# First expert weight blocks in half-block buffers, and another order of the last pieces and the second norm

## The chip, the core and the metric

One program on one core of a Trainium2 chip. The metric is the device time of one execution in microseconds (us). The engines are PE (TensorE, with PEld its weight loads), DVE (VectorE), ACT (ScalarE), POOL (GpSimd) and SP (SyncE, which here only issues transfers).

## What is computed

One layer of a hybrid encoder on 512 tokens of width 1024, in float32: three token mixers (chunk-band attention, gated delta rule, causal pooling), gated, merged and projected; a residual sum and a layer norm; then a mixture of experts, a residual sum and a second layer norm. The change touches only the second half:

```python
x = layer_norm(DN_ALPHA * x + mix, ln1_g[i], ln1_b[i])
ffn = hierarchical_moe(x, ...)      # top group of 4, then top 2 of its 8 experts, per token
x = layer_norm(DN_ALPHA * x + ffn, ln2_g[i], ln2_b[i])

def expert_block(args):             # 32 experts; w1, w3: 1024x512, w2: 512x1024
    xb, e = args
    hdn = jax.nn.silu(xb @ w1[e]) * (xb @ w3[e])
    return hdn @ w2[e]

def layer_norm(x, g, b):
    mu = jnp.mean(xf, axis=-1, keepdims=True)
    var = jnp.mean(jnp.square(xf - mu), axis=-1, keepdims=True)
    return ((xf - mu) * lax.rsqrt(var + LN_EPS) * g + b)
```

## The kernel before

**The expert stage.** All 32 experts are computed, each for up to 64 tokens that chose it. They are taken in 16 pairs; the two experts of a pair stand in the two 64-column halves of the PE array. The tokens of four experts are gathered by matmuls with one-hot matrices (`gather`, group "g" in the profile). Per pair there are three products: with w1 and with w3 (`first_product`, 8 chunks of the contraction by 2 experts, output `as`), silu and multiplication (`gated`), four transposes of the result (`turned_slots`, output `g`), and with w2 (`product`, output `pj`). Each float32 matmul of these stands in the trace as two, so one first product is 32 rows and one second product 32 rows of 512 columns or 64 of 256. The loop over the pairs runs w1 of pair `pr`, then w2 of pair `pr - 1`, then w3 of pair `pr`.

**The weights.** One expert matrix is a block of 2 MB; there are 96 blocks, and a pair uses two blocks per product. They pass through eight slots of one block each, in one fixed arena of on-chip memory. Every buffer in the program is a name for a range of that arena (`reg(offset, size)`), and two names may overlap. `seq` holds the order of use: blocks 0 and 1 are w1 of pair 0, 2 and 3 its w3, 4 and 5 w1 of pair 1, 6 and 7 w2 of pair 0, 8 and 9 w3 of pair 1, and so on. `load_expert` issues blocks 0 to 5 as one transfer each, blocks 7 and 8 in quarters, `load_quarter` block 6 in quarters; these go out while the mixers still run. From block 9 on `load_parts` issues half a block (1 MB, line 1098) or a whole one (2 MB, line 1094) into whatever `done_with` has declared free. In pairs 0 to 2 a slot's first half is declared free in the middle of a product, after chunk 4 of 8, or for w2 after the second of four 256-column pieces (`PIECES`).

**What sets the order.** From `held(True)` on, PE, ACT and DVE each run strictly in the order in which the program text issues; SP issues its transfers in one queue in the order of issue, each after its own waits. Waits come from overlaps: a read of a buffer waits for earlier writes to any buffer that overlaps it.

**The end.** Pairs 13 to 15 are not written out, but combined on chip: `product` leaves a high part (ACT) and a low part (DVE, `m_512r` or `m_1024r`), `combine` multiplies both with a token matrix and adds the result to the residual `yacc`, for four token tiles. For pair 15 that addition also gives the row sum of each 256-column piece, and a pass with Square gives its sum of squares: on ACT, and for the last piece of tiles 2 and 3 on DVE. `gained(k)` multiplies piece `k` by the norm's gain in place. `second_scale(t)` makes mean and 1/deviation of one tile (nine small instructions on three engines), `second_norm(t)` applies them and stores the rows.

```python
def block(i):                        # before: blocks 0 to 5
    return lambda c: reg(slot(i), 8, 512)[:, c]
```

Of the kernel before, what the change touches and what calls it, by code (L numbers as in the profile page):

```python
# [14 lines left out]
AF = mybir.ActivationFunctionType  # L15
OP = mybir.AluOpType
# [145 lines left out]
def body(tc, T):  # L162
# [24 lines left out]
    pool, sp = nc.gpsimd, nc.sync  # L187
# [9 lines left out]
    def reg(off, *dims, r=False):  # L197

        n = math.prod(dims)
        key = (off, n, r)  # L200
        if key not in placed:
            name = "m%d_%d%s" % (off, n, "r" if r else "")
            placed[key] = nc.alloc_sbuf_tensor_at(name, [128, n], F32R if r else F32, offset=base + 4 * off)
        v = placed[key][:, 0:n]
        return shaped(v.bitcast(F32) if r else v, *dims)

    def shaped(v, *dims):
        if len(dims) == 1:
            return v
        names = "abcd"[:len(dims)]  # L210
        kw = {names[i]: dims[i] for i in range(len(dims) - 1)}
        return v.rearrange("p (%s) -> p %s" % (" ".join(names), " ".join(names)), **kw)

    r32 = lambda v: v.bitcast(F32R)

    def pt(tag, bufs, *dims):
        t = ps.tile([128, 512], F32, name=tag, tag=tag, bufs=bufs)
        if not dims:
            return t
        return shaped(t[:, :math.prod(dims)], *dims)  # L220
# [39 lines left out]
    ident = C["ident"]  # L260
# [765 lines left out]
    def slot(i):  # L1026

        return YHL[0] if i == 0 else YO if i == 6 else slots[i - 1 - (i > 6)]

    def quarter(i, k):  # L1030

        return reg(RING[2] + 1024 * k if i == 7 else woh[1][k], 1024)
# [6 lines left out]
    def block(i):  # L1039

        if seq[i][0] == "moe_w2":
            if i == 7:
                return lambda f, cs: shaped(quarter(i, cs.start // 256), 4, 256)[:, f]
            if i > 8:
                return lambda f, cs: w2_columns(shaped(half(i, cs.start // 512), 2, 4, 256), f,
                                                slice(cs.start % 512, cs.start % 512 + cs.stop - cs.start))
            return lambda f, cs: w2_columns(reg(slot(i), 4, 4, 256), f, cs)
        if i == 8:
            return lambda c: quarter(i, c // 2)[:, c % 2 * 512:c % 2 * 512 + 512]
        if i > 8:  # L1050
            return lambda c: shaped(half(i, c // 4), 4, 512)[:, c % 4]
        return lambda c: reg(slot(i), 8, 512)[:, c]

    def blocks(pr):
# [18 lines left out]
    def half(i, h):  # L1073

        p = place_of[i]
        return reg(p[0], 4096)[:, 2048 * h:2048 * h + 2048] if i in whole else reg(p[h], 2048)
# [48 lines left out]
    def load_expert(i=None):  # L1125
        if i is None:
            i = nl_[0]
            nl_[0] += 1
        if i == 8:

            for p in range(4):
                for k in (7, 8):
                    sp.dma_start(quarter(k, p), T[seq[k][0]][seq[k][1]][:, 1024 * p:1024 * p + 1024])
        elif i < 6:
            sp.dma_start(reg(slot(i), 4096), T[seq[i][0]][seq[i][1]])

    def load_quarter(t):

# [392 lines left out]
    def combine(pr, cs, PT_, ws):  # L1531

        n = cs.stop - cs.start
        pcs = [pt(*((("pj", 3), ("ao", 1), ("pj", 3), ("g", 2)) if pr == 13 else
                    (("as", 2), ("ao", 1), ("as", 2), ("g", 2)))[t])[:, :n] for t in range(4)]

        for t in range(4):
            for i, v in enumerate(outs(pr, cs)):
                pe.matmul(pcs[t], r32(PT_[:, t]), r32(v), start=(i == 0), stop=(i == 1))
            ya, pc = yacc[:, t, cs], pcs[t]  # L1540
            if pr < 15:
                dve.tensor_tensor(ya, ya, pc, op=OP.add)
            else:

                k = cs.start // n
                dve.scalar_tensor_tensor(ya, pc, 1.0, ya, op0=OP.mult, op1=OP.add, accum_out=bnp[:, t, k, 1:2])
                if k == 3 and t > 1:
                    d = sil[1][:, (t % 2) * n:(t % 2) * n + n]
                    dve.tensor_scalar(d, ya, -float(n), bnp[:, t, k, 1:2], op0=OP.mult, op1=OP.add)
                    dve.scalar_tensor_tensor(d, d, 1.0, d, op0=OP.mult, op1=OP.mult, accum_out=bnp[:, t, k, 2:3])  # L1550
                else:
                    act.activation(junk[:, :n], ya, AF.Square, scale=-float(n), bias=bnp[:, t, k, 1:2],
                                   accum_out=bnp[:, t, k, 2:3])

    def gained(k, ts=range(4)):

        for t in ts:
            ya = yacc[:, t, PIECES[k]]
            dve.tensor_tensor(ya, ya, late["g2"][:, PIECES[k]], op=OP.mult)
# [14 lines left out]
    bnp = bns.rearrange("p t a b -> p t (a b)")[:, :, 0:3 * len(PIECES)].rearrange("p t (k b) -> p t k b", b=3)  # L1574
    junk = sil[0]

    def second_scale(t):

        ms, rows2 = late["ms"], late["rows"]
        dve.bn_aggr(mv[:, t], bnp[:, t].rearrange("p a b -> p (a b)"))  # L1580
        act.activation(mv[:, t, 1:2], mv[:, t, 1:2], AF.Sqrt, scale=256.0 ** -2, bias=eps[:, 1:2])
        yield
        m, d = mv[:, t, 0:1], mv[:, t, 1:2]
        dve.reciprocal(d, d)
        dve.tensor_scalar(r32(ms[:, t, 0:3:2]), m.to_broadcast([128, 2]), d, None, op0=OP.mult)
        dve.tensor_scalar(ms[:, t, 1:2], m, d, ms[:, t, 0:1], op0=OP.mult, op1=OP.subtract)
        p = pt("g", 2)[0:5, 0:128]
        pe.transpose(p, ms[:, t, 0:5], ident)
        act.activation(r32(rows2[:, t]), p, AF.Copy)
        yield  # L1590

    def second_norm(t):

# [54 lines left out]
    for pr in range(16):  # L1648
# [15 lines left out]
        if 0 < pr < 15:  # L1664
            for cs in PIECES if pr == 1 else halves:
                product(pr - 1, cs, blocks(pr - 1)[4:], *turned_.get(pr - 1, ()))
                if pr < 3 and cs.stop == 512:
                    done_with(pr - 1, "moe_w2", hs=(0,))
            done_with(pr - 1, "moe_w2", hs=(1,) if pr < 3 else (0, 1))
            if pr < 14:  # L1670
                put_rows(pr - 1)
            else:
                for cs in halves:
                    combine(pr - 1, cs, *turned_[pr - 1])
# [46 lines left out]
    dve.memset(late["ms"][:, :, 3:5], 1.0)  # L1721
    last[2]()
    next(rows_)
    combine(14, halves[1], *turned_[14])
    next(rows_)
    last[3]()
    combine(15, PIECES[0], *turned_[15])
    last[4]()
    combine(15, PIECES[1], *turned_[15])
    gained(0)  # L1730
    last[5]()
    combine(15, PIECES[2], *turned_[15])
    gained(1)
    combine(15, PIECES[3], *turned_[15])
    scales = [second_scale(t) for t in range(4)]
    for t in range(6):
        if t < 4:
            next(scales[t])
        if 0 < t < 5:
            next(scales[t - 1])  # L1740
        if t < 4:
            gained(2, (t,))
            gained(3, (t,))
        if t > 1:
            second_norm(t - 2)
    ctx.close()


# [14 lines left out]
```

## Time and profile before

| what | value |
|---|---|
| runs | 1113.26, 1115.53, 1116.07 us; median 1115.53 |
| profiled execution | 1114.25 us, span of the trace 1112.5 us |
| mean granted PE clock | 0.956 of full |
| busy in the span | PE 1010.5 us (91%), DVE 467.2, ACT 310.1, POOL 193.1 |
| HBM read | 254.67 MB |

The page of the profile has busy time by engine, slices of the span, transfer queues, the chain that ended last and groups of instructions. "Idle before, releaser" is the time an engine stood before an instruction and what ended that wait. The granted clock is the share of its full rate that PE was given; 1.0 is 2.4 GHz and 0.5 is 1.2 GHz. The DMA share is the mean busy share of the core's 16 transfer engines. Line 182 (and 180) is a helper through which all PE, DVE and ACT instructions go.

### The profile page before, as it was taken

The page shows a single profiled execution, that of the slowest core. Times are in us where ns is not written, and L with a number is a line of the kernel's source. Part 1 is how long each engine was busy: PE and PEld are TensorE (multiplying, and loading weights), DVE is VectorE, ACT ScalarE, POOL GpSimd, SP SyncE. Part 2 cuts the span into 40 slices and gives each one's busy share as a digit, 9 for nine tenths or more (in the row PEclk, how much of TensorE's full clock was granted, in tenths as well). Part 3 has the DMA queues.
Part 4 walks back from the last instruction along what each step waited for, and adds up shares of the span by engine and source line. Part 5 has one row for each costly group of instructions (what it writes and reads, how often), then busy time and mean ns, then how long its engine had stood idle before and what let it go on. Part 6 is the DMA issues. An engine that isn't in the chain of part 4 may idle for free. (4 is left out here: it accounts for less than half of the span.)

```text
span 1112.5 us, 13291 instructions
## 1 busy us (share of the span) xinstructions
PE 1010.5 (91%) x5174; PEld 647.9 (58%) x5174; DVE 467.2 (42%) x1010; ACT 310.1 (28%) x651; POOL 193.1 (17%) x182
## 2 busy tenths in 40 slices
PE   8989996999999999999976599989899899988893
PEld 5778785977677888887761253525243453523352
DVE  6766993257744524434660111141111152122647
ACT  6883332255743223342240010101010010100023
POOL 1631650132330101331230000000012000001000
PEclk9999998999999999999987899999999899998986
DMA  9422314311114233344663769999999999999952
GB/s 350 141 85 67 114 38 114 108 32 52 39 42 156 107 114 132 152 152 175 265 229 121 295 241 411 425 426 428 428 425 427 428 425 422 426 425 426 417 243 76
DMA packets 44354, 266.40 MB, mean 239 GB/s; under 512 B 15096, under 2 KB 15608, under 8 KB 24448
## 3 DMA queue, kind: packets, MB, share of 16 engines
q1 hardware_dynamic: 39920, 254.53, 57.3%
q0 software_dynamic: 3504, 8.49, 2.0%
q10 hardware_dynamic: 864, 2.49, 0.7%
q8 instruction: 42, 0.69, 0.2%
q14 instruction: 24, 0.20, 0.0%
HBM read 254.67 MB, written 14.09 MB: 242 GB/s over the span
## 5 line engine op out<-in xcount | busy, mean ns | idle before, releaser
L182 PE MATMUL as<-m,m 128*64 128x512 f32 x1024 | 253.7, 627 | 32.3 <-DMA m<-moe_w 31.5
L180 PE MATMUL pj<-m_4096r,m_1024r 128*128 128x512 f32 x800 | 253.1, 396 | 0.0
L182 PEld LDWEIGHTS as<-m,m 128*64 128x64 f32 x1024 | 76.0, 144 | 186.9 <-issue 140.9
L180 PE MATMUL pj<-m_4096r,m_2048r 128*128 128x512 f32 x448 | 170.1, 397 | 9.7 <-ACT m_2048r L180 5.5
L180 PEld LDWEIGHTS pj<-m_4096r,m_1024r 128*128 128x128 f32 x800 | 147.0, 188 | 33.8 <-issue 4.5
L182 PE MATMUL pj<-m,m 128*64 128x512 f32 (+1 forms) x608 | 122.9, 546 | 10.8 <-DMA m<-moe_w 10.8
L180 ACT ACTIVATE m_1024r<-m 128x512 fp32r<-128x512 f32 (+1 forms) x90 | 78.2, 869 | 145.2 <-PE pj L180 120.4
L180 DVE TENSOR_TENSOR m_2048r<-m,m_1024r 128x1024 fp32r<-128x1024 f32 x67 | 76.4, 1141 | 97.7 <-ACT m_1024r L180 97.6
L180 PEld LDWEIGHTS pj<-m_4096r,m_2048r 128*128 128x128 f32 x448 | 85.0, 190 | 29.6 <-ACT m_2048r L180 5.5
L182 PEld LDWEIGHTS pj<-m,m 128*64 128x64 f32 x608 | 48.4, 143 | 80.8 <-issue 68.7
L180 PE MATMUL g<-m,m 128*128 128x128 f32 (+5 forms) x472 | 68.7, 281 | 14.8 <-DMA m<-dx 11.0
L182 DVE COPY m<-pj 128x512 f32<-128x512 f32 (+1 forms) x14 | 9.1, 653 | 172.8 <-PE pj L182 172.8
L1511 POOL DMA_INDIRECT yd<-m,m x13 | 12.6, 968 | 373.2 <-DVE m L182 339.4
L180 PEld LDWEIGHTS g<-m,m 128*128 128x128 f32 (+3 forms) x472 | 58.6, 173 | 27.9 <-issue 16.0
L182 DVE TENSOR_TENSOR m<-m,as 128x512 f32<-128x512 f32 x20 | 13.7, 686 | 139.9 <-PE as L182 139.9
L182 ACT ACTIVATE m<-g 128x512 f32<-128x512 f32 x16 | 9.6, 597 | 176.1 <-PE g L182 176.1
L182 PE MATMUL g<-m_1024r,m_4096r 128*128 128x256 f32 x224 | 55.0, 287 | 0.0
L182 PE MATMUL g<-m_1024r 128*128 128x256 f32 x224 | 54.0, 283 | 0.0
L783 POOL TENSOR_SCALAR m<-m,m 128x128 f32<-128x128 f32 (+3 forms) x32 | 36.6, 1152 | 90.8 <-DVE m L180 84.9
L180 PE MATMUL pj<-m_1024r,m_4096r 128*128 128x512 f32 (+1 forms) x204 | 50.4, 391 | 0.6 <-ACT m_4096r L180 0.6
L182 ACT ACTIVATE m<-g,m 128x256 f32<-128x256 f32 x28 | 15.8, 564 | 116.7 <-PE g L182 116.7
L182 PEld LDWEIGHTS g<-m_1024r,m_4096r 128*128 128x128 f32 x224 | 42.9, 191 | 7.3 <-issue 6.5
(205 smaller groups left out, 1263.8 us busy)
## 6 DMA issues: line engine op xcount, KB each, us to landing
m<-moe_w SPq DMA_DIRECT2D x70, 2048.0 KB, 22.9
m<-moe_w SPq DMA_DIRECT2D x44, 1024.0 KB, 18.3
m<-wm SPq DMA_DIRECT2D x33, 1024.0 KB, 4.9
m<-moe_w SPq DMA_DIRECT2D x16, 512.0 KB, 6.0
yd<-m SPq DMA_DIRECT2D x4, 1024.0 KB, 8.3
m<-wo SPq DMA_DIRECT2D x2, 2048.0 KB, 10.2
m<-yd POOLq DMA_DIRECT2D x8, 512.0 KB, 29.7
m<-xT SPq DMA_DIRECT2D x8, 256.0 KB, 6.2
```

Of the source, the lines that this page charges most:

```text
L180: return f(*args, **kw)
L182: r = f(*args, **kw)
L783: pool.tensor_scalar(s_[:, :n], s_[:, :n], st[:, 1:2], None, op0=OP.mult)
L1511: pool.indirect_dma_start(out=yd, out_offset=bass.IndirectOffsetOnAxis(ap=tabs.bitcast(I32)[:, pr, 0:1], axis=0), in_=ybf[pr], in_offset=N ...
```

## The change

It has five parts. (1) Blocks 1 to 5 are loaded as two transfers of 1 MB into two buffers of half a block, and read through these names. (2) The two w2 blocks of pair 0 are declared free in one go after the last of the four pieces; before, their first halves after the second piece. (3) At the end, the second half of `combine(14)` moves from before the second piece of pair 15 to after the first `gained`; the last piece's product moves behind the third piece's `combine`; `gained(2)` is done for all tiles before the last piece. (4) The squares of the last piece of tiles 2 and 3 move from DVE to ACT. (5) The scales of the second norm are made for all four tiles in one set of instructions.

```diff
@@ block(i)
+        if i:
+            return lambda c: reg(slot(i) + 2048 * (c // 4), 4, 512)[:, c % 4]
         return lambda c: reg(slot(i), 8, 512)[:, c]
@@ load_expert
+        elif i == 0:
+            sp.dma_start(reg(slot(i), 4096), T[seq[i][0]][seq[i][1]])
         elif i < 6:
-            sp.dma_start(reg(slot(i), 4096), T[seq[i][0]][seq[i][1]])
+            for h in range(2):
+                sp.dma_start(reg(slot(i) + 2048 * h, 2048), T[seq[i][0]][seq[i][1]][:, 2048 * h:2048 * h + 2048])
@@ combine, pair 15
-                if k == 3 and t > 1:
-                    d = sil[1][:, (t % 2) * n:(t % 2) * n + n]
-                    dve.tensor_scalar(d, ya, -float(n), bnp[:, t, k, 1:2], op0=OP.mult, op1=OP.add)
-                    dve.scalar_tensor_tensor(d, d, 1.0, d, op0=OP.mult, op1=OP.mult, accum_out=bnp[:, t, k, 2:3])
-                else:
-                    act.activation(junk[:, :n], ya, AF.Square, scale=-float(n), bias=bnp[:, t, k, 1:2],
-                                   accum_out=bnp[:, t, k, 2:3])
+                act.activation(junk[:, :n], ya, AF.Square, scale=-float(n), bias=bnp[:, t, k, 1:2],
+                               accum_out=bnp[:, t, k, 2:3])
@@ second_scale(t) becomes second_scales()
+        for t in range(4):
+            dve.bn_aggr(mv[:, t], bnp[:, t].rearrange("p a b -> p (a b)"))
+        m, d = mv[:, :, 0:1], mv[:, :, 1:2]
+        act.activation(d, d, AF.Sqrt, scale=256.0 ** -2, bias=eps[:, 1:2])
         dve.reciprocal(d, d)
+        dve.tensor_tensor(r32(ms[:, :, 0:3:2]), m.to_broadcast([128, 4, 2]), d.to_broadcast([128, 4, 2]), op=OP.mult)
+        dve.tensor_tensor(ms[:, :, 1:2], m, d, op=OP.mult)
+        dve.tensor_tensor(ms[:, :, 1:2], ms[:, :, 1:2], ms[:, :, 0:1], op=OP.subtract)
+        p = pt("g", 2, 4, 128)
+        for t in range(4):
+            pe.transpose(p[0:5, t], ms[:, t, 0:5], ident)
+        act.activation(r32(rows2), p[0:5], AF.Copy)
@@ loop over pairs
-                if pr < 3 and cs.stop == 512:
+                if pr == 2 and cs.stop == 512:
                     done_with(pr - 1, "moe_w2", hs=(0,))
-            done_with(pr - 1, "moe_w2", hs=(1,) if pr < 3 else (0, 1))
+            done_with(pr - 1, "moe_w2", hs=(1,) if pr == 2 else (0, 1))
@@ the end
     next(rows_)
-    combine(14, halves[1], *turned_[14])
+    last[3]()
     next(rows_)
-    last[3]()
     combine(15, PIECES[0], *turned_[15])
     last[4]()
     combine(15, PIECES[1], *turned_[15])
     gained(0)
-    last[5]()
+    combine(14, halves[1], *turned_[14])
     combine(15, PIECES[2], *turned_[15])
     gained(1)
+    gained(2)
+    last[5]()
     combine(15, PIECES[3], *turned_[15])
-    scales = [second_scale(t) for t in range(4)]
...
+    gained(3)
+    second_scales()
+    for t in range(4):
+        second_norm(t)
```

The first place is PE in the w1 product of pair 0, chunks 3 to 5. A name like `m27648_4096_62` is a buffer at offset 27648 of 4096 elements, number 62; `m14336_4096_109` is block 0, the buffer at 27648 (and 29696) block 1, and `DMAHW6_49` the semaphore of a transfer. Before:

```order
L182 MATMUL as_4355<-m14336_4096_109,m20480_2048_121 64x512 [waits Activation_49]
L182 MATMUL as_4355<-m27648_4096_62,m20480_2048_121 64x512
L182 MATMUL as_4355<-m14336_4096_109,m20480_2048_121 64x512 [waits DVE_49]
L182 MATMUL as_4355<-m27648_4096_62,m20480_2048_121 64x512 [waits DMAHW6_49]
L182 MATMUL as_4355<-m14336_4096_109,m20480_2048_121 64x512 [waits Activation_49]
L182 MATMUL as_4355<-m27648_4096_62,m20480_2048_121 64x512
```

and with the change:

```order
L182 MATMUL as_4360<-m14336_4096_109,m20480_2048_121 64x512 [waits Activation_49]
L182 MATMUL as_4360<-m27648_2048_134,m20480_2048_121 64x512
L182 MATMUL as_4360<-m14336_4096_109,m20480_2048_121 64x512 [waits DVE_49]
L182 MATMUL as_4360<-m29696_2048_3744,m20480_2048_121 64x512 [waits DMAHW2_49]
L182 MATMUL as_4360<-m14336_4096_109,m20480_2048_121 64x512 [waits Activation_49]
L182 MATMUL as_4360<-m29696_2048_3744,m20480_2048_121 64x512
```

At chunk 4 the matmul on block 1 waited on semaphore 6; now it reads a buffer of its own, at 29696, and waits on semaphore 2, that of the transfer that fills it.

To the same place belongs SP's queue at the loads from block 9 on, as it stood before. A transfer waits for the last user of the semaphore that it takes:

```order
L1098 DMA m18432_2048_110<-moe_w3 128x2048 [waits DMAHW4_49]
L1140 DMA m10240_4096_173<-moe_w2 128x1024 [waits DVE_49,DMAHW5_49,PE_49,Pool_49]
L1098 DMA m27648_2048_134<-moe_w3 128x2048 [waits DMAHW6_49,PE_49]
L1098 DMA m48128_2048_314<-moe_w1 128x2048 [waits DMAHW7_49,PE_49]
L1098 DMA m44032_2048_63<-moe_w1 128x2048 [waits DMAHW0_49,PE_49]
L1098 DMA m50176_2048_3243<-moe_w1 128x2048 [waits DMAHW1_49,PE_49]
```

Semaphore 6 belongs to the third row, the second half of block 9, which goes into offset 27648, the first half of block 1's slot. The next rows (semaphores 7, 0, 1) are halves of blocks 10 and 11 into the slots of blocks 2 and 3. With the change the same six rows stand there in the same order.

The second place is SP's queue at the first expert loads. Before:

```order
L278 DMA m48128_2048_314<-wm 128x2048 [waits DMAHW7_49,DVE_49,PE_49]
L278 DMA m44032_2048_63<-wm 128x2048 [waits DMAHW0_49,DMAHW6_49,DVE_49,PE_49]
L1135 DMA m48128_4096_3744<-moe_w3 128x4096 [waits DMAHW4_49,DVE_49,PE_49]
L1135 DMA m27648_4096_62<-moe_w1 128x4096 [waits DMAHW2_49,PE_49,Pool_49]
L1135 DMA m44032_4096_3746<-moe_w3 128x4096 [waits DMAHW3_49,DMAHW6_49,DVE_49,PE_49]
L1135 DMA m35840_4096_3291<-moe_w1 128x4096 [waits DMAHW1_49,DVE_49,PE_49]
```

and with the change:

```order
L278 DMA m48128_2048_314<-wm 128x2048 [waits DMAHW7_49,DVE_49,PE_49]
L1140 DMA m50176_2048_3243<-moe_w3 128x2048 [waits DMAHW6_49,DVE_49,PE_49]
L278 DMA m44032_2048_63<-wm 128x2048 [waits DMAHW0_49,DVE_49,PE_49]
L1140 DMA m48128_2048_314<-moe_w3 128x2048 [waits DMAHW1_49,DMAHW4_49,DVE_49,PE_49]
L1140 DMA m29696_2048_3744<-moe_w1 128x2048 [waits DMAHW2_49,Pool_49]
L1140 DMA m27648_2048_134<-moe_w1 128x2048 [waits PE_49]
L1140 DMA m46080_2048_233<-moe_w3 128x2048 [waits DMAHW3_49,DMAHW5_49,DVE_49,PE_49]
L1140 DMA m44032_2048_63<-moe_w3 128x2048 [waits DMAHW6_49,DMAHW7_49,DVE_49,PE_49]
```

Ten half loads stand in the place of five whole ones, and the second half of block 2 (offset 50176) now stands ahead of the last mixer weights (line 278, offset 44032).

The third place is DVE at the end, from the sum of a piece on. `m_4096_173` is `yacc`; the additions of `as`, `ao`, `as`, `g` over 128x512 are the second half of `combine(14)`, those over 128x256 with a second output a piece of pair 15, and the 128x256 products with `m_1024_4241` (`m_1024_4246`) are `gained`. Before:

```order
L182 TENSOR_TENSOR m_4096_173<-m_4096_173,as 128x512
L182 TENSOR_TENSOR m_4096_173<-m_4096_173,ao 128x512
L182 TENSOR_TENSOR m_4096_173<-m_4096_173,as 128x512
L182 TENSOR_TENSOR m_4096_173<-m_4096_173,g 128x512
L182 SCALAR_TENSOR_TENSOR m_1024r<-m_1024r,m_2048_60,m_1024_4245 5x1024
L182 SCALAR_TENSOR_TENSOR m_1024r<-pj,m_976_61,m_1024r 128x256
L182 SCALAR_TENSOR_TENSOR m_4096_173,m_976_61<-as,m_4096_173 128x256
L182 SCALAR_TENSOR_TENSOR m_4096_173,m_976_61<-ao,m_4096_173 128x256
L182 SCALAR_TENSOR_TENSOR m_4096_173,m_976_61<-as,m_4096_173 128x256
L182 SCALAR_TENSOR_TENSOR m_4096_173,m_976_61<-g,m_4096_173 128x256
L182 SCALAR_TENSOR_TENSOR m_1024r<-pj,m_976_61,m_1024r 128x256
L182 SCALAR_TENSOR_TENSOR m_4096_173,m_976_61<-as,m_4096_173 128x256
```

and with the change:

```order
L182 TENSOR_TENSOR m_4096_173<-m_4096_173,m_1024_4246 128x256 x4
L182 TENSOR_TENSOR m_4096_173<-m_4096_173,as 128x512
L182 TENSOR_TENSOR m_4096_173<-m_4096_173,ao 128x512
L182 TENSOR_TENSOR m_4096_173<-m_4096_173,as 128x512
L182 TENSOR_TENSOR m_4096_173<-m_4096_173,g 128x512
L182 SCALAR_TENSOR_TENSOR m_4096_173,m_976_61<-as,m_4096_173 128x256
L182 SCALAR_TENSOR_TENSOR m_4096_173,m_976_61<-ao,m_4096_173 128x256
L182 SCALAR_TENSOR_TENSOR m_4096_173,m_976_61<-as,m_4096_173 128x256
L182 SCALAR_TENSOR_TENSOR m_4096_173,m_976_61<-g,m_4096_173 128x256
L182 TENSOR_TENSOR m_4096_173<-m_4096_173,m_1024_4246 128x256 x8
L182 SCALAR_TENSOR_TENSOR m_1024r<-pj,m_976_61,m_1024r 128x256
L182 SCALAR_TENSOR_TENSOR m_4096_173,m_976_61<-as,m_4096_173 128x256
```

The four additions of `combine(14)` stood ahead of the low part of the second piece; now they stand between the first `gained` and the third piece, and eight `gained` products stand ahead of the low part of the last piece.

## Rows read from the trace of the kernel before

**Rows 1.** Page, part 2: DMA busy share in 40 slices of 27.8 us.
```profile
DMA  9422314311114233344663769999999999999952
```

**Rows 2.** Two stretches: length, busy us by engine, granted clock, DMA share, GB/s.
```profile
581.90:651.40 69.50, 48.12 (x198) 17.66 (x197) 6.09 (x20) 4.39 (x8) 2.59 (x3) 0.80 0.53 201
651.40:1060.30 408.90, 379.04 (x1890) 167.92 (x1888) 102.00 (x240) 40.46 (x72) 26.75 (x30) 0.97 0.99 418
```

**Rows 3.** Timeline of PE from the first expert product: start, us, work, idle before and releaser.
```profile
581.88 4.50 PE L182 MATMUL as<-m,m 128*64 128x512 f32 x18
...
590.60 9.51 PE L182 MATMUL as<-m,m 128*64 128x512 f32 x30 [4.21 <-DMA m<-moe_w]
...
638.61 5.97 PE L182 MATMUL pj<-m,m 128*64 128x256 f32 x32 [6.77 <-DMA m<-moe_w]
...
651.38 0.39 PE L182 MATMUL g<-m_1024r,m_4096r 128*128 128x256 f32 x1
```

**Rows 4.** PE's waits from 582 to 645 us: total, times, longest.
```profile
PE as L182 <- DMA m<-moe_w: 14.6, 5, 5.3
PE pj L182 <- DMA m<-moe_w: 6.8, 1, 6.8
```

**Rows 5.** Timeline of SP's queue: issues of expert weights, start us and us.
```profile
585.58 0.33 SPq L1098 DMA_DIRECT2D m<-moe_w  x1
...
599.29 0.33 SPq L1098 DMA_DIRECT2D m<-moe_w  x1
...
667.08 0.33 SPq L1094 DMA_DIRECT2D m<-moe_w  x1
```

**Rows 6.** DMA issues: mixer weights, KB each, median us from issue to landing.
```profile
m<-wm SPq DMA_DIRECT2D x33, 1024.0 KB, 4.9
```

**Rows 7.** Expert loads issued from 599 to 667 us, by line.
```profile
L1098 SPq DMA_DIRECT2D m<-moe_w x14: 327/328/383, 599.3 to 651.5; - x14
L1094 SPq DMA_DIRECT2D m<-moe_w x1: 683/683/683, 651.9 to 651.9; - x1
```

**Rows 8.** Timeline of PE: transposes, half a first product, a second product, undisturbed.
```profile
662.82 0.66 PE L182 MATMUL g<-m,m 128*128 128x128 f32 x4
663.40 3.65 PE L182 MATMUL as<-m,m 128*64 128x512 f32 x16
666.89 7.04 PE L182 MATMUL pj<-m,m 128*64 128x512 f32 x32
```

**Rows 9.** Two stretches as in Rows 2: half loads alone, and the full stream.
```profile
630.00:640.00 10.00, 3.23 (x22) 1.96 (x21) 0.42 (x1) 0.38 (x1) 0.00 (x0) 0.82 0.96 385
...
700.00:800.00 100.00, 91.53 (x466) 39.94 (x464) 22.19 (x80) 10.15 (x18) 2.89 (x3) 0.98 1.01 427
```

**Rows 10.** SP's queue: last mixer weights, and block 2.
```profile
475.00 0.33 SPq L278 DMA_DIRECT2D m<-wm  x1
...
491.32 0.33 SPq L1135 DMA_DIRECT2D m<-moe_w  x1
```

**Rows 11.** Timeline of DVE: last piece's first sum, first aggregate, the last norms.
```profile
1092.70 0.42 DVE L182 SCALAR_TENSOR_TENSOR m<-as,m 128x256 f32<-128x256 f32 x1
...
1095.79 0.21 DVE L182 BATCH_NORM_AGGREGATE m<-m 128x2 f32<-128x12 f32 x1
...
1099.92 1.41 DVE L182 SCALAR_TENSOR_TENSOR m<-m,m,pj 128x512 f32<-128x512 f32 x2 [0.53 <-PE pj L182]
...
1106.48 2.72 DVE L182 SCALAR_TENSOR_TENSOR m<-m,m,pj 128x512 f32<-128x512 f32 x4 [1.19 <-PE pj L182]
```

**Rows 12.** Groups by form, 1075 to 1110 us, DVE and ACT: busy us, mean ns.
```profile
L182 DVE TENSOR_TENSOR m<-m,m 128x256 f32<-128x256 f32 x16 | 5.8, 415 | 0.0
...
L182 DVE TENSOR_TENSOR m<-m,as 128x512 f32<-128x512 f32 x2 | 1.3, 668 | 0.0
...
L182 ACT ACTIVATE m<-m,m 128x256 f32<-128x256 f32 x14 | 7.1, 509 | 6.2 <-DVE m L182 5.6
...
L182 ACT ACTIVATION_READ_ACCUMULATOR m<-m,m 128x1 f32 x14 | 2.6, 186 | 0.0
```

More of the change, by code (lines that the diff above doesn't have):

```diff
@@ L1575, in body, with second_scales @@
     junk = sil[0]
-    def second_scale(t):
+    def second_scales():
         ms, rows2 = late["ms"], late["rows"]
[L1580 to L1583, printed above, removed]
+        for t in range(4):
+            dve.bn_aggr(mv[:, t], bnp[:, t].rearrange("p a b -> p (a b)"))
+        m, d = mv[:, :, 0:1], mv[:, :, 1:2]
+        act.activation(d, d, AF.Sqrt, scale=256.0 ** -2, bias=eps[:, 1:2])
         dve.reciprocal(d, d)
[L1585 to L1590, printed above, removed]
+        dve.tensor_tensor(r32(ms[:, :, 0:3:2]), m.to_broadcast([128, 4, 2]), d.to_broadcast([128, 4, 2]), op=OP.mult)
[5 more added lines that the diff above has]
+        act.activation(r32(rows2), p[0:5], AF.Copy)
     def second_norm(t):
@@ L1730, in body @@
     gained(0)
-    last[5]()
+    combine(14, halves[1], *turned_[14])
     combine(15, PIECES[2], *turned_[15])
     gained(1)
+    gained(2)
+    last[5]()
     combine(15, PIECES[3], *turned_[15])
-    scales = [second_scale(t) for t in range(4)]
[L1736 to L1745, printed above, removed]
+    gained(3)
+    second_scales()
+    for t in range(4):
+        second_norm(t)
     ctx.close()
```

## The prediction

> **What bounds the kernel now.** I read the slices of the page first, then the windows, then the timelines of PE and SP. The row of DMA shares [rows 1] shows where to look: from slice 24 (667 us) the transfers fill every slice until the tail, and just ahead of that stand three slices at 0.3, 0.7 and 0.6 (584 to 667 us), in which expert weights are loaded as well. The windows say the same with PE beside it [rows 2]. From 651.4 to 1060.3 us the DMA share is 0.99 at 418 GB/s, and PE works 379.0 of 408.9 us: the stream of weight blocks sets the pace, and PE follows it closely. From 581.9 to 651.4 us neither is full: PE works 48.1 of 69.5 us at a granted clock of 0.80, and the DMA share is 0.53 at 201 GB/s. So whatever this stretch loses is lost for good, because the full stream behind it has no slack in which to make it up.
>
> Why nothing is full there, the timeline of PE tells [rows 3]: from the first expert matmul at 581.88 it stands again and again for weights, 4.21 us at 590.60 and 6.77 us at 638.61 for instance. The totals are 14.6 us in five waits and 6.8 us in one, together 21.4 us [rows 4]. The odd thing is what PE waits for. At 585.58 SP issues a half load [rows 5], in the middle of w1 of pair 0; 4.9 us is what 1 MB takes from issue to landing when little else is under way [rows 6], which gives 590.5, and PE goes on at 590.60. The load is the second half of block 9, and the order shows why PE minds: it goes into the first half of block 1's slot, while PE is about to read the second half of that slot under the name of the whole block. The wait is false; block 1 has long been there. Its cost is double: while PE waits, it frees no slots, so SP has nothing to issue (the next one comes at 599.29), and the stream stands as well.
>
> **Parts 1 and 2: the false waits.** With half-block names every matmul in chunks 4 to 7 waits for its own load alone, and since the w2 blocks of pair 0 are freed in one go, no new load goes into them while they are read. PE's path from 581.9 to the gather, now at 651.38 [rows 3], is then: w1 of pair 0, w3 of pair 0, w1 and w3 of pair 1 at two halves of 3.65 us, less a small overlap, 7.1 each; one product at 7.04; four transposes at 0.66 [rows 8]. That is 4 x 7.1 + 7.0 + 0.7 = 36.1 us, so the gather starts at 618.0 and **PE is 33.4 us earlier**. That takes these durations at the clock of the later stretch. If I take instead PE's own 48.1 busy us of this stretch and only bring them from clock 0.80 to 0.97 [rows 2], they are 39.7 us, and PE is 29.8 us earlier. Rows 8 are single undisturbed pieces of the same shapes, the other end holds rows that straddle waits; I take the middle, 31.6, and keep both ends.
>
> PE alone decides nothing if the stream cannot follow. SP's next issue, the first half of block 10, comes after chunk 4 of w3 of pair 0: 581.9 + 7.1 + 3.6 = 592.6, in the place of 599.29. From there to the whole block issued at 667.08 [rows 5] the loads are 14 halves and one whole block, 16 units of 1 MB [rows 7]. At the 427 GB/s of the full stream [rows 9] one takes 2.46 us. The first flows 4.9 - 2.46 = 2.4 us after its issue; 16 units are 39.3 us, and one write of a pair's rows (0.5 MB) is 1.2 us more. The stream is through with them at 592.6 + 2.4 + 39.3 + 1.2 = 635.5. In between PE frees four units each at about 596, 604, 611 and 618, always ahead of the transfers. In the trace of before the block issued at 667.08 meets an empty queue and flows at 669.5: so the stream could be **34.0 us earlier**, a little more than PE. The smaller decides: 31.6 us, with bounds 29.8 and 33.4. As a check, the stretch moved 201 GB/s x 69.5 us = 14.0 MB, 32.7 us at 427 GB/s, so a PE path of 36 us does not ask more of the stream than it has given.
>
> From 651.4 to 1060.3 I add nothing: PE and the stream both move as a whole, by nearly the same amount, and the shares 0.99 and 0.93 of that stretch remain. Blocks 1 to 5 as halves cost ten issues of 0.33 us on SP for five of 0.68 [rows 7]; SP is idle there, and the slices from 473 to 528 us, when these blocks load, are at 0.4 [rows 1], so this is hidden.
>
> **SP's queue.** One half of block 2 now stands ahead of the last mixer weights, which were issued at 475.00; block 2 as a whole went at 491.32 [rows 10]. If its second half came free only then, the mixer weights would be 16.3 us late, and all that follows with them: that is the upper end. The lower is nothing. A queue that is blocked delays only what has no slack, and the offset at stake held weights that were loaded ahead of the one at 48128, so it should be free within a few us; I take nothing, and keep a small case for it.
>
> **Parts 3 to 5: the tail.** From the first sum of the last piece, 1092.70, to the end of the last norm (1106.48 + 2.72) it is 16.5 us [rows 11]. After the change this is: the first sum, 0.4; four squares on ACT at 0.51 + 0.19, 2.8 us [rows 12], with DVE's sums beside them; the chain from the first aggregate to the first norm, 1095.79 to 1099.92, 4.1 us [rows 11], once for all tiles; eight norms at 0.68, 5.4 us [rows 11]. Sum 12.7; I put 0.3 on it, since three-dimensional scales are somewhat longer: 13.0, so 3.5 us less. Against that, four additions of `combine(14)` and four `gained` now stand ahead of the first sum: 4 x 0.6 + 4 x 0.36 = 3.8 us [rows 12]. PE also does the second half of `combine(14)` later, so the pieces' products come earlier and half of the 3.8 should be covered: 2.0 us. Net **-1.5 us**. If all is covered and the chain is shorter by the squares on DVE as well, it is about -4; if nothing is covered and the four squares queue behind those of the third piece, +2.5.
>
> **The sum.** The profiled execution takes 1114.25 us: 1114.25 - 31.6 - 1.5 = 1081.2. It lies 1.3 us under the median of the runs, so the forecast for the median is **1082.5 us**. The bounds give 1078 to 1088.
>
> **Rivals.**
> *Slower refill.* The transfers from 593 to 636 us are halves, and of halves alone the trace has 385 GB/s, at a share of 0.96 [rows 9]; 1 MB is then 2.72 us, 14 of them cost 3.7 us more, and up to two handovers at which the queue runs dry cost 2.4 each. Against it: that stretch has gaps, and with units queued behind each other the gaps close. The stream's 34.0 becomes 30.3 to 25.5: 1083.7 to 1088.5, some 1087. The Trainium skill, page "DMA: Bandwidth & Descriptors", section Bandwidth, speaks against smaller transfers here: it advises batching and gives 341 GB/s for 1 MB, far under its larger ones. By that figure 1 MB is an estimated 3.07 us, the 14 cost 8.6, and the time is about 1089 to 1093. The trace of this case disagrees, with 385 GB/s at the same size in a stretch not quite full.
>
> *Only the stalls are saved.* If the clock stays at 0.80 in the stretch, PE keeps its 48.1 us [rows 2], and only the 21.4 us of waits go [rows 4]: 1115.5 - 21.4 - 1.5 = 1092.6. For it: the clock was low through the whole stretch, also in work between waits. Against it: 0.98 in the full stretch where PE works 91.5 of 100 us [rows 9]; without waits PE works as densely here.
>
> *SP blocked at the mixer weights.* Up to 16.3 us [rows 10] are lost: up to 1099, still faster.
>
> *Slower: the clock falls in the long stretch.* PE, now nearer to the stream, would wait in short pieces more often, and at 0.80, as it was given between 581.9 and 651.4 [rows 2], it would become the bound. Its 379.0 us at 0.97 are 368 at full rate. From the gather at 618.0 to 1060.3 there are 442.3 us, so even if all idle time vanished it would be slower than before from a clock of 0.83 downwards; at 0.80 PE needs 460, and the end is at 1115.5 + 17 - 1.5 = 1131. For it speaks only that 0.80 occurs beside waits; against it, that the same mix of work and waits behind 651.4 has 0.97 throughout.
>
> *The waits stay.* If some other name still overlaps, the gain is the tail's alone: 1114. The order of PE speaks against it: chunk 4 waits for semaphore 2, its own load.
>
> **How the numbers follow.** Chances: forecast 0.70, slower refill 0.14, only the stalls 0.08, SP blocked 0.03, the waits stay 0.02, slower 0.03. The range: the forecast's own, 1078 to 1088, widened down by 2 us for a clock that is full at once, and up to 1093 to take in the refill and part of the stalls. About 3.3 us (0.3%) is what a measurement of this kernel can tell from no change; all cases but the last two are beyond that: faster 0.95, same 0.02, slower 0.03.
>
> **What would show it.** In the profile of the changed kernel PE has no wait for weights from 582 to 618 us, its clock there is 0.9 or more, and the gather behind w3 of pair 1 starts at about 618 to 622. SP issues the half of block 10 at about 592.6; the whole block now at 667.08 goes at about 634 to 637. The DMA slices are at nine tenths from about 600 us. The first sum of the last piece to the last norm takes about 13 us. Wrong would be: a DMA rate under 400 GB/s between 595 and 635; a gather later than 625; PE waits for other loads in its place; a last mixer load issued after 480; or a clock under 0.9 behind 651.

## The result, and the profile after

The changed kernel takes 1080.67 us (median of four runs, 1079.50 to 1082.29) beside 1115.53 us for the kernel before; the ratio is 0.9694 with an interval of 0.9670 to 0.9717, some 34 us. A fourth run of the kernel before, at 1447.63 us, is a slow one and is left out. The profiled execution took 1081.32 us, with a span of 1079.6 us. The page of the changed kernel, part 2, answers to [rows 1]; its slices are 27.0 us long:

```profile
DMA  8422223311113223445455999999999999999962
```

The full stream now begins in slice 22, counted from 0 (594 us), instead of slice 24 (667 us). The windows from the first expert product to the gather behind w3 of pair 1, and from there to w3 of pair 15, answer to [rows 2] (columns as there):

```profile
583.97:619.51 35.54, 35.54 (x198) 14.01 (x197) 6.12 (x20) 4.41 (x8) 2.60 (x3) 0.99 0.78 314
619.51:1029.23 409.72, 379.51 (x1890) 167.07 (x1888) 102.06 (x240) 40.58 (x72) 26.75 (x30) 0.97 1.01 424
```

The same 198 rows of PE that took 48.12 us within 69.50 us now take 35.54 us within 35.54 us. So the stretch lost not only its 21.4 us of waits: the work itself became 12.6 us shorter. Some 9 us of this is the granted clock, 0.80 in the window before and 0.99 now (an estimate: each piece of the 48.12 us, taken at its own granted clock, makes 38.6 us at the full rate, where 35.54 us at 0.99 make 35.2). The other 3.4 us the clock does not explain. Some of them lie in rows right behind a wait, such as these two of the kernel before, which took 1.97 us at a granted clock of 0.50, where a row of the long piece shown next takes 0.22 us at 0.98:

```profile
604.25 1.97 PE L182 MATMUL as<-m,m 128*64 128x512 f32 x2 [4.15 <-DMA m<-moe_w]
```

The second window is as long as before, 409.7 us against 408.9, with the DMA share at 1.01.

PE's timeline of the changed kernel (start, us, work) answers to [rows 3], [rows 8]:

```profile
583.97 17.66 PE L182 MATMUL as<-m,m 128*64 128x512 f32 x80
...
605.63 7.08 PE L182 MATMUL pj<-m,m 128*64 128x256 f32 x64
612.54 7.04 PE L182 MATMUL as<-m,m 128*64 128x512 f32 x32
619.51 0.39 PE L182 MATMUL g<-m_1024r,m_4096r 128*128 128x256 f32 x1
```

Two and a half first products run as one piece of 80 rows, and no row has a wait (the window above has PE busy for all of its 35.54 us). SP's issues answer to [rows 5], [rows 10]: two loads of mixer weights, the first half of block 10, and the whole block that stood at 667.08.

```profile
444.03 0.34 SPq L278 DMA_DIRECT2D m<-wm  x1
...
476.67 0.33 SPq L278 DMA_DIRECT2D m<-wm  x1
...
594.79 0.33 SPq L1100 DMA_DIRECT2D m<-moe_w  x1
...
635.22 0.33 SPq L1096 DMA_DIRECT2D m<-moe_w  x1
```

DVE's end answers to [rows 11]: the last piece's first sum, the aggregates of all tiles at once, the eight norms in a row.

```profile
1062.64 0.42 DVE L182 SCALAR_TENSOR_TENSOR m<-as,m 128x256 f32<-128x256 f32 x1 [0.48 <-PE as L182]
...
1066.05 0.42 DVE L182 BATCH_NORM_AGGREGATE m<-m 128x2 f32<-128x12 f32 x4
...
1070.08 5.35 DVE L182 SCALAR_TENSOR_TENSOR m<-m,m,pj 128x512 f32<-128x512 f32 x8 [2.58 <-PE pj L182]
```

Four points of each trace divide the time: F, PE's first expert product; G, the gather behind w3 of pair 1; W, PE's start of w3 of pair 15; E, the end of the last norm on DVE (start plus us of its row). The time in us:

| kernel | F at | F to G | G to W | W to E | F to E |
|---|---|---|---|---|---|
| before | 581.88 | 69.50 | 408.96 | 48.86 | 527.32 |
| changed | 583.97 | 35.54 | 409.72 | 46.20 | 491.46 |
| changed, again | 583.92 | 35.57 | 410.47 | 45.85 | 491.89 |
| parts 3 to 5 alone | 583.56 | 70.20 | 408.60 | 46.24 | 525.04 |
| parts 1 and 2 alone | 582.79 | 35.39 | 409.91 | 48.55 | 493.85 |
| without part 2 | 583.84 | 49.84 | 408.98 | 45.46 | 504.28 |
| even and odd chunks | 582.96 | 60.49 | 408.34 | 46.35 | 515.18 |
| whole blocks, freed at the end | 582.26 | 35.36 | 412.63 | 46.36 | 494.35 |
| halves, declared free at the end | 582.14 | 35.33 | 410.23 | 45.83 | 491.39 |
| late read | 583.26 | 37.61 | 406.66 | 47.81 | 492.08 |
| halves to the end | 581.95 | 35.34 | 413.48 | 46.31 | 495.13 |
| squares on DVE | 583.85 | 35.53 | 410.72 | 46.73 | 492.98 |
| old order | 583.08 | 35.52 | 409.86 | 45.57 | 490.95 |
| products first | 582.83 | 35.49 | 409.74 | 43.51 | 488.74 |

F lies between 581.88 and 583.97 in programs that are alike up to there in nearly everything, so about 2 us of a single execution is scatter from ahead of the change; F to E is free of it. The changed kernel, its repetition and "halves, declared free at the end" (which turned out to be the same schedule) agree in F to E within 0.5 us. The scatter of F begins early: of the 2.1 us between the kernel before and the changed one, 1.3 are there at 20 us, behind 48 matmuls that took 12.61 us in the one and 13.70 in the other. The stretches scatter as well: G to W is 409.7 to 410.7 us in the seven kernels that are alike up to W (the three named, "parts 1 and 2 alone", "squares on DVE", "old order", "products first").

### The profile page after: what moved, and what is told of

Same layout as the page of the kernel before. It is cut to its first block, busy times and chain, and to the rows that moved or that the text cites. A ratio compares the mean times of both kernels' runs of the same rounds, so it can differ in the third digit from the quotient of the medians.

```text
span 1079.6 us, 13289 instructions
## 1 busy us (share of the span) xinstructions
PE 1002.4 (93%) x5174; PEld 647.8 (60%) x5174; DVE 463.9 (43%) x996; ACT 310.5 (29%) x649; POOL 194.7 (18%) x182
## 5 line engine op out<-in xcount | busy, mean ns | idle before, releaser
L182 PE MATMUL as<-m,m 128*64 128x512 f32 x1024 | 244.0, 614 | 16.2 <-DMA m<-moe_w 15.3
L182 PE MATMUL pj<-m,m 128*64 128x512 f32 (+1 forms) x608 | 119.9, 537 | 6.1 <-DMA m<-moe_w 6.1
L182 PEld LDWEIGHTS pj<-m,m 128*64 128x64 f32 x608 | 45.9, 140 | 76.7 <-issue 60.9
L1516 POOL DMA_INDIRECT yd<-m,m x13 | 12.6, 966 | 339.9 <-DVE m L182 334.7
```

The costliest lines, as they stand in the source:

```text
L182: r = f(*args, **kw)
L1516: pool.indirect_dma_start(out=yd, out_offset=bass.IndirectOffsetOnAxis(ap=tabs.bitcast(I32)[:, pr, 0:1], axis=0), in_=ybf[pr], in_offset=N ...
```

## The experiments

**The parts apart.** Parts 3 to 5 alone: `block`, `load_expert` and the w2 release as before the change.

> Parts 3 to 5 alone, with the expert blocks as before the change. Theory: 1.8 us less than before, about 1114.0 us, with PE's waits of 21.4 us between 582 and 645 us as before. Rival (the end only pays in the changed kernel): the same as before, 1115.8, or slower.

Measured: 1112.97 us, ratio 0.9978 (0.9968 to 0.9987). The theory holds, with 2.5 us (1.5 to 3.6) rather than 1.8. Its waits for weights are those of before (14.8 and 7.1 us). Parts 1 and 2 alone, with the end as before:

> Parts 1 and 2 alone, with the end as it was before. Theory (the false waits are nearly all of the gain, and the parts add up): the stretch from the first expert product to the gather behind w3 of pair 1 is 35.5 us as in the changed kernel, the time is 1.8 us above the changed kernel, about 1082.5 us. Rival (much of the gain came from the end of the program): 1090 us or more.

Measured: 1084.16 us, ratio 0.9715 (0.9698 to 0.9731), 1.7 us over the theory's figure and far from the rival's; F to G is 35.39 us. The gain is in the blocks: 33.5 us of F to E (527.32 - 493.85), and 2.3 us for the end alone (527.32 - 525.04); together 35.8, and 35.9 in the changed kernel. The parts add up.

**The wait in w2, by itself.**

```diff
-                if pr == 2 and cs.stop == 512:
+                if pr < 3 and cs.stop == 512:
                     done_with(pr - 1, "moe_w2", hs=(0,))
-            done_with(pr - 1, "moe_w2", hs=(1,) if pr == 2 else (0, 1))
+            done_with(pr - 1, "moe_w2", hs=(1,) if pr < 3 else (0, 1))
```

> The changed kernel, but with the w2 blocks of pair 0 freed by halves in the middle again (without part 2). Theory: the new half load of block 14 goes into the block that PE reads, behind eight units that are already queued; it lands at about 619.3 us, PE stands 10 us in w2 of pair 0 and frees the next slots later, and the stream runs dry: about 10 us above the changed kernel, 1089 to 1092 us. Rival 1: the wait is as long as before, 6.8 us, and the stream hides it: within 2 us of the changed kernel. Rival 2: the loads are far enough ahead that the wait is gone without part 2: 1080.7.

Measured: 1091.99 us, ratio 0.9781 (0.9764 to 0.9797). PE's timeline of this kernel, the second half of w2 of pair 0:

```profile
620.52 6.37 PE L182 MATMUL pj<-m,m 128*64 128x256 f32 x32 [11.09 <-DMA m<-moe_w]
```

and its window from F to G:

```profile
583.84:633.68 49.84, 38.75 (x198) 15.79 (x197) 6.12 (x20) 4.40 (x8) 2.60 (x3) 0.85 0.71 280
```

The theory holds in place and in price. The wait is longer than the 6.8 us of before because the stream is no longer empty when the new load is issued. It goes out at 609.46 and lands 10.9 us later, behind four half loads (issued from 601.83 to 606.42) that have not landed when it goes; the expectation had eight. Without part 2, part 1 would have kept a third of the loss.

**Whole blocks, freed late.** If the overlap is the cause, it must be possible to avoid it with whole blocks too: names and loads of before, but slots of blocks 0 to 5 declared free only at the end of a product.

```diff
             if c == 4:
-                if pr < 3:
+                if pr < 3 and place[pr, name, 0] > 5:
                     done_with(pr, name, hs=(0,))
...
-            done_with(pr, "moe_w1", hs=(1,) if pr < 3 else (0, 1))
+            done_with(pr, "moe_w1", hs=(1,) if pr == 2 else (0, 1))
...
-            done_with(pr, "moe_w3", hs=(1,) if pr < 3 else (0, 1))
+            done_with(pr, "moe_w3", hs=(1,) if 0 < pr < 3 else (0, 1))
```

> Blocks 1 to 5 whole in load and name as before the change, but their slots are declared free only after the last chunk. Theory (overlapping names cost the time, not the size of the loads): PE has no wait for weights from the first expert product to the gather, 35.5 us as in the changed kernel. The first half of block 10 goes out 3.4 us later, and since the stream then ends its 16 units later than PE needs them, the time is 3.4 us above the changed kernel, about 1084 us. Rival 1 (PE alone sets the shift, the stream has slack): the same as the changed kernel, 1080.7. Rival 2 (half loads are needed): the waits are back, 1110 us or more.

Measured: 1082.21 us, ratio 0.9699 (0.9683 to 0.9715). SP's issue of the first half of block 10, and the window from F to G:

```profile
596.34 0.33 SPq L1098 DMA_DIRECT2D m<-moe_w  x1
```
```profile
582.26:617.62 35.36, 35.36 (x197) 14.00 (x196) 6.12 (x20) 4.39 (x8) 2.60 (x3) 1.00 0.70 275
```

No wait, full clock, with loads of 2 MB: half loads are not needed, only names that no new load overlaps. That rival is out. The issue is 14.1 us behind F, in the changed kernel 10.8 us (594.79 - 583.97); so the stream starts 3.3 us later, and F to E is 2.5 to 3.0 us longer. The intervals of the times overlap with those of the changed kernel; in the traces F to E lies outside its scatter of 0.5 us, and G to W (412.6) outside the 409.7 to 410.7 of the kernels alike. The same edit on the changed kernel, with half loads and half names:

> The changed kernel, but with the slots of blocks 0 to 5 declared free only after the last chunk. Theory: the same as the run with whole blocks freed at the end, about 1084 us, with 0 to 0.5 us between the two; so all that the half names are worth over a later release is 3.4 us. Rival (half loads themselves make the stream faster or slower): 3 us or more between the two.

Measured: 1079.59 us, ratio 0.9677 (0.9661 to 0.9694). This run did not do what its expectation says. Block 10 goes out at 592.75, 10.6 us behind F, as in the changed kernel: `done_with` only decides where in the program text a load stands; when it goes, its waits decide, and with half names these end with the last read of that half. So it says nothing on a late release, and is one more run of the changed schedule.

**Later start with half loads.** To free halves late in truth, each half of blocks 1 to 5 was given every second chunk:

```diff
-            return lambda c: reg(slot(i) + 2048 * (c // 4), 4, 512)[:, c % 4]
+            return lambda c: reg(slot(i) + 2048 * (c % 2), 4, 512)[:, c // 2]
...
-                sp.dma_start(reg(slot(i) + 2048 * h, 2048), T[seq[i][0]][seq[i][1]][:, 2048 * h:2048 * h + 2048])
+                sp.dma_start(reg(slot(i) + 2048 * h, 4, 512),
+                             T[seq[i][0]][seq[i][1]].rearrange("p (c h n) -> p c h n", h=2, n=512)[:, :, h])
```

> The changed kernel, but the two halves of blocks 1 to 5 hold the even and the odd chunks, so that both halves are read until the end of a product and neither comes free early; loads and names stay halves. Theory (the stream has only about 1 us of slack behind PE, so a start 3.5 us later costs 2 to 3 us, whatever the size of the loads): from the gather behind w3 of pair 1 to w3 of pair 15 it is 412 to 413 us, as with whole blocks freed at the end (412.6), and the time is 1082 to 1083.5 us. Rival (what the whole blocks lost came from the size of their loads or from scatter): 409.7 to 410.5 us there as in the changed kernel, 1080.5 us.

Measured: 1104.71 us, ratio 0.9896 (0.9881 to 0.9911). Neither came: the early `done_with` at chunk 4 still stands ahead of chunks 4 and 6 in the text, so here PE takes the new block's data for these chunks and waits for them. PE's waits from 582 to 650 us (total, times, longest):

```profile
PE as L182 <- DMA m<-moe_w: 13.2, 5, 5.1
```

As a test of the late start it is void, and its result is not the layer's. Its times still tell something else: the five waits in first products are back, that of w2 is not. F to E is 23.7 us longer than in the changed kernel; the w2 wait alone made 12.8; together 36.5, beside 33.6 for both in one kernel (525.04 - 491.46). The two kinds of waits nearly add up, and those in first products are about two thirds.

**Later start by another read.**

```diff
+        if pr == 1:
+            p = pt("g", 2)
+            for i in (2, 3):
+                for c in (0, 4):
+                    pe.matmul(p[0:64, 0:64], XGs[0][:, 1, 0, 0:64], block(i)(c)[:, 0:64], start=True, stop=True)
```

> The changed kernel with four small matmuls more behind w1 of pair 1 that read blocks 2 and 3 once again (their result is used nowhere), so that the first half of block 10 goes out 11 us later, with all that stands behind it in SP's queue; PE itself loses under 1 us. Theory (the stream decides as soon as its 1 us of slack is gone): 9 to 11 us more than the changed kernel between the gather and w3 of pair 15, about 1090 us. Rival (PE sets the shift and the stream catches up): within 2 us of the changed kernel, 1080.5 to 1082.

Measured: 1081.45 us, ratio 0.9685 (0.9672 to 0.9698). For the same reason this did not delay SP (block 10 at 593.96, 10.7 us behind F); the reads, standing behind the loads in the text, waited for them. What it did was to hold PE:

```profile
606.84 0.27 PE L182 MATMUL g<-m,m 128*64 128x64 f32 x1 [1.53 <-DMA m<-moe_w]
```

F to G is 37.6 us, 2.1 more than in the changed kernel, and F to E as a whole only 0.2 to 0.7 more. So its expectation's case was not tested. It looks as if PE could lose 2 us in this stretch for nothing, but the delay was not absorbed on the way. PE waits for weights in w1 of pair 15, some 20 us ahead of W. The row behind that wait, in the kernel before, in the changed kernel, with the late read and with the whole blocks:

```profile
1040.99 3.65 PE L182 MATMUL as<-m,m 128*64 128x512 f32 x14 [1.23 <-DMA m<-moe_w]
1010.11 3.65 PE L182 MATMUL as<-m,m 128*64 128x512 f32 x14 [1.55 <-DMA m<-moe_w]
1011.20 3.65 PE L182 MATMUL as<-m,m 128*64 128x512 f32 x14 [2.56 <-DMA m<-moe_w]
1011.16 3.65 PE L182 MATMUL as<-m,m 128*64 128x512 f32 x14 [1.39 <-DMA m<-moe_w]
```

Measured from each kernel's own F it starts at 459.1, 426.1, 427.9 and 428.9 us; in the seven kernels alike up to W it lies between 425.8 and 426.3. So the late read is still 1.7 to 2.1 us late there, and the whole blocks 2.6 to 3.1. What the late read won back it won behind that row. In the changed kernel the granted clock is 0.50 in the last 3.3 us ahead of W and 0.85 in the w3 product behind it; with the late read it is 1.00 in both, the seven matmuls ahead of W take 1.78 us instead of 3.28, and PE stands 2.20 us for DVE ahead of them instead of 3.48. That is no slack in the stretch; why the clock held at the end is not shown.

**The size of the loads.** All loads up to block 89 in halves: `range(2) if i < 90` in `parts`.

> The changed kernel with all loads up to block 89 in halves of 1 MB, in the place of whole blocks of 2 MB from block 17 on. Theory (a half load costs the queue nothing when others are queued behind it; the 385 GB/s were gaps): the stream stays at 424 to 427 GB/s and the time within 2 us of the changed kernel. Rival 1 (halves run at 385 GB/s): the stream from 636 to 1040 us is 10% longer, about 1120 us. Rival 2 (the Trainium skill, page DMA: Bandwidth & Descriptors, section Bandwidth, has 341 GB/s for 1 MB): by that figure an estimated 25% longer, about 1180 us.

Measured: 1085.20 us, ratio 0.9729 (0.9713 to 0.9744). The window from 700 to 800 us of this kernel:

```profile
700.00:800.00 100.00, 89.78 (x454) 40.31 (x452) 19.87 (x74) 10.17 (x18) 2.88 (x3) 1.00 1.01 421
```

and of the changed kernel, with whole blocks:

```profile
700.00:800.00 100.00, 89.27 (x436) 38.56 (x436) 21.96 (x80) 9.58 (x17) 3.08 (x4) 0.97 1.01 427
```

Both rivals are out by far, and the theory by a little: a half load does cost something, 1.4% of the rate, and 3 to 4 us over the 410 us from G to W. 385 GB/s was a matter of gaps, not of size.

**The end.** The changed kernel once more, beside three variants:

> The changed kernel once more, beside the variants of its end on the same chip: 1080.7 us, within 1.5 us; from the start of w3 of pair 15 to the end of the last norm 46.2 us.

Measured: 1080.23 us, ratio 0.9681 (0.9667 to 0.9694); W to E 45.85 us. Squares of the last piece of tiles 2 and 3 on DVE, as before the change:

> The changed kernel without part 4: the squares of the last piece of tiles 2 and 3 are on DVE again. Theory: ACT loses 1.4 us from its chain of four squares, DVE gains 1.6 us; the two nearly cancel, so 0 to 0.8 us slower than the changed kernel at the end of the last norm. Rival (ACT's four squares in a row were a cost of the change): 1 us faster.

Measured: 1081.65 us, ratio 0.9694 (0.9681 to 0.9707); W to E 46.73, 0.5 to 0.9 us more. The sign is the theory's, but in the nine kernels that have the end of the change W to E lies between 45.46 and 47.81 us (47.81 with the late read, where W is early; 46.36 at most in the others). So neither the trace nor the times tell the two apart with certainty; of the rival, 1 us faster, nothing is seen. The order of the pieces as before the change:

> The changed kernel with the order of the last pieces as before (without part 3), squares on ACT and scales together as in the change. Theory (the new order costs 1.1 us at the first sum of the last piece, and the joint scales gain 3.7 us behind it): from the start of w3 of pair 15 to the end of the last norm 45.2 us, 1 us less than the changed kernel. Rival (the order is what pays): 48 us, 2 us more.

Measured: 1080.85 us, ratio 0.9684 (0.9671 to 0.9697); W to E 45.57, 0.3 to 0.6 us less. The sign is the theory's, the size is within scatter; the rival is out. Part 3 brings nothing that can be seen, and part 4 at most 0.9 us; so what the end gains should come from the joint scales of part 5, which were not run by themselves. Last, a better order:

```diff
     next(rows_)
-    combine(15, PIECES[0], *turned_[15])
     last[4]()
+    combine(15, PIECES[0], *turned_[15])
     combine(15, PIECES[1], *turned_[15])
     gained(0)
+    last[5]()
     combine(14, halves[1], *turned_[14])
     combine(15, PIECES[2], *turned_[15])
     gained(1)
-    gained(2)
-    last[5]()
     combine(15, PIECES[3], *turned_[15])
-    gained(3)
+    gained(2)
     second_scales()
...
@@ second_scales
+        gained(3)
         p = pt("g", 2, 4, 128)
         for t in range(4):
             pe.transpose(p[0:5, t], ms[:, t, 0:5], ident)
```

> Another order of the end on top of the change: the products of the last two pieces issue ahead of the combinations that they stand behind now, and the last gained products go under the scales' chain. Theory (DVE idles 2.2 us for ACT's high part, which stands behind squares, and 2.6 us ahead of the last norms; both can be filled): 3 to 4 us less at the end, about 1077 us. Rival (DVE's own work sets the end): within 1 us of the changed kernel.

Measured: 1077.46 us, ratio 0.9657 (0.9642 to 0.9672), beside 1080.23 for the changed kernel on the same chip; W to E is 43.51, 2.3 to 2.7 us less, where 3 to 4 were expected. It is the fastest of all, and the rival is out. DVE's rows show which idle went and which stayed:

```profile
1053.84 0.48 DVE L182 SCALAR_TENSOR_TENSOR m_1024r<-pj,m,m_1024r 128x256 fp32r<-128x256 f32 x1 [1.98 <-ACT m_1024r L182]
...
1066.21 5.36 DVE L182 SCALAR_TENSOR_TENSOR m<-m,m,pj 128x512 f32<-128x512 f32 x8 [1.24 <-PE pj L182]
```

Ahead of the norms 1.24 us of idle time are left of 2.58, since the last `gained` products lie in it; the wait for ACT's high part, 2.18 us in the changed kernel, has only moved to the last piece, where eight squares now stand ahead of it.

## Why the prediction held, step by step

**The cause: right.** PE's waits were for loads that had nothing to do with what it read. The whole blocks freed late show it by another way than the change's: no overlap, no wait, whatever the size of a load. That the waits also starved the stream is seen in SP's queue: block 10 is issued 10.8 us behind F instead of 17.4 (599.29 - 581.88), and the block of 667.08 at 635.22.

**PE's path: under-sized.** The forecast had 36.1 us by undisturbed pieces and 39.7 by bringing the stretch's own busy time to clock 0.97, and took the middle. The path is 35.54 us: the first end was right, and 34.0 us were gained where 31.6 stood. The second end failed less by the clock, 0.99 instead of 0.97, which would make it 38.9, than by what its 48.1 busy us held: the 3.4 us beyond the clock in the work beside waits. The forecast had seen that this end "holds rows that straddle waits", and took the middle all the same. The Trainium skill says on its page "TensorE: Matmul & The Clock Gate", Part 1, that the throttled state is the default and activity releases it; the rows agree, 0.80 with 21.4 us of waits in the stretch, 0.85 with 11.1 and 0.99 with none.

**"The smaller decides": not settled.** The forecast had PE 33.4 and the stream 34.0 us earlier at best and let PE decide. From F, the gather came 34.0 us earlier, and the row behind the wait in w1 of pair 15 33.0 (459.1 against 426.1). With PE 2.1 us later that row came 1.7 to 2.1 later, with the stream 3.3 us later 2.6 to 3.1. Each delay passed on nearly whole, so neither PE nor the stream had as much as 1 us to spare. Which of the two sets the pace stays open: a PE that is held also frees its slots later (with the late read SP issues the block of 667.08 at 636.58, 2.1 us later behind F than in the changed kernel), and the three runs that were to delay the stream alone, with half loads, did not. For the time it matters little, since the two are so close.

**Nothing between 651.4 and 1060.3: nearly.** G to W is 0.8 to 1.5 us longer; with scatter of this size nothing further is claimed.

**SP's queue: right at nothing.** The last mixer weights go at 476.67 instead of 475.00; but a load ahead of it, which no edit touches, is as much later, 444.03 instead of 442.36. SP's queue of the kernel before has that row:

```profile
442.36 0.34 SPq L278 DMA_DIRECT2D m<-wm  x1
```

Both moved by 1.67 us, so the half of block 2 between them cost nothing.

**The end: direction right, size short.** From the first sum of the last piece to E it is 12.8 us (1062.64 to 1075.43); the forecast was 13.0, from 16.5. The first sum comes 1.1 us later against W, where the forecast had 2.0. So W to E is 2.7 us shorter instead of 1.5; of this 0.9 us is lost behind E, where the span ends 4.2 us after the last norm instead of 3.3, and all tiles' rows now go out together.

**The sum.** For the profiled execution 1081.2 was forecast and 1081.32 came. That is closer than its terms: 34.0 from the stretch, 1.8 from the end, less 0.8 behind G and 2.1 at F make 32.9, where the forecast had 31.6 + 1.5 = 33.1. The 2.1 at F is scatter, and hid what was under-sized: that the single execution was hit to 0.1 us is luck. Without it the terms make 35.0, and the medians differ by 34.9 (34.1 by the ratio); the median came 1.8 us under the forecast of 1082.5.

**The rivals.** Slower refill: out. From 595 to 635 us, where the refill is nearly all halves, it ran at 410 GB/s; the stream ran at 424 from G on, and halves throughout at 421. The Trainium skill's 341 GB/s for 1 MB ("DMA: Bandwidth & Descriptors", Bandwidth) is far from all three; its table is of transfers issued from GpSimd, and these are issued from SP. Only the stalls: out, the work itself gave back another 12.6 us, some 9 of them by the clock. What spoke for it, a clock that is low through the whole stretch, also misread the trace of before: the granted clock was 1.00 from 581.88 to 586.38 and again from 644.40 to 651.38, and 0.50 from 604.25 to 606.73. A falling clock in the long stretch: out, 0.97 as before. SP blocked, waits that stay: out.

## What to carry to other kernels

When a transfer is issued early into half of a buffer that is still being read, look at the name under which the other half is read: if that name covers the new transfer's range, the reader waits for data that it does not want, and if the reader also frees the buffers, the transfers starve with it. Where the text of the program sets the dependencies, an early release has to stand behind the last read of that range in the text, and a later release in the text does not by itself make a transfer later. In a stretch of waits, price the work beside the waits as well: here it was 12.6 us beside 21.4, some 9 of them by the clock. And compare a delay at a row far ahead of the end before calling it free.

## What was not expected of the hardware

The same 198 rows of PE took 48.12, 38.75 and 35.54 us at granted clocks of 0.80, 0.85 and 0.99, in the kernel before, without part 2 and in the changed kernel; work of the same rows cost up to a third more beside waits of up to 6.8 us, and some 9 of the 12.6 us between the first and the last are the clock. Near the end the same seven matmuls, which no edit touches, took 3.28 us at a granted clock of 0.50 in the changed kernel and 1.78 at 1.00 with the late read. And loads of 1 MB, queued one behind another, ran at 421 GB/s where loads of 2 MB ran at 427: a loss of 1.4%, not of a tenth.
